# State-space outputs beside the gate projections, five recurrence steps a round, and another order in the gate

## The chip, the cores and the metric

The kernel runs on one core of one Trainium2 chip. The metric is device time in microseconds of one execution; the median of three runs is compared. Everything is float32 at the borders; products run on TensorE with each operand split into a high and a low part in a reduced float format, three matmuls for one product.

## The reference

A block with pooling and sparse attention comes first, then a gated linear attention layer, then the state-space layer that this change touches (S = 1024 positions, inner width 2048 as 128 groups of 16 channels, 64 complex states a group):

```python
u, z = split(h @ w_in)                      # 2048 columns each
states = scan(lam_bar * state + B_bar u)    # 128 groups, 64 complex states, 1024 steps
y = Re(C states) + d_skip * u
y = gelu(y)
y = y * sigmoid(y @ w_glu + b_glu)
y = y * silu(z)
out = y @ w_out
```

## The kernel before

The sequence is cut into 128 chunks of 8 positions, and the 128 groups into 16 octets of 8 groups (`octet(o)`). For each octet four small matrices do the work: `w_mat` takes the inputs of a chunk to the state that the chunk adds, `kp_d` (the T pieces) gives the outputs that depend on the chunk's own inputs, the recurrence carries states over the 128 chunks, and `v_mat` takes the carried state to outputs. The tile `X` holds the states: 64 KB a partition, indexed by state (real and imaginary parts on the 128 partitions), chunk and group, so that one octet's elements for one chunk are 8 contiguous floats and the next chunk lies 512 bytes on.

The weights, the inputs and the states all come through one stream, `WStream` (lines 43 to 144). A piece is put in order, loaded by SyncE into one of three raw buffers, and split by `pump`: ScalarE casts the high part (L177), VectorE or GpSimd (`lo`) subtracts for the low part (L185). Split pieces stand in a ring of six, are taken in the order in which they were put, and are freed by `release`. A piece with a gate is not started before its gate is true. All engines take their instructions in the order written; nothing is reordered.

`s5` (L2125) has these stages.

- The first loop, 19 rounds. Round i projects columns i of `w_in` (`project`: 48 matmuls 512 wide in two halves, evacuated by ScalarE at L2154) and, from round 3 on, does octet i - 3 (`states`: 24 matmuls 128 wide with `w_mat`, evacuated into `X` at L2196, then 24 with T, evacuated at L2204 and stored in `yp_d`). Rounds 16 to 18 already project the first three column blocks of z, with SiLU in the evacuation, stored in `z_d`.
- The recurrence, a generator on VectorE (`scan`, L2213) for four octets at a time, 29 steps each: three that only wait for a load, 15 over chunks within a segment, 4 that carry the ends of segments, 7 that correct a segment each. `scan_on(n)` writes n steps into the program; the first loop writes 4 a round from round 7 on.
- The second loop, 13 rounds, the other column blocks of z: one projection and `scan_on(6)` each. The products with `v_mat` come after it.
- The third loop, 16 rounds, one octet each. It takes a `v_mat` piece and the split states of the octet (the `X` piece), does 24 matmuls 128 wide into a two-bank PSUM tile (`big`, two of them), adds the stored part (VectorE, L2361), does the GELU (ScalarE, L2366), and for the octet two rounds back `y_out`: 8 transposes (L2316) into two PSUM banks, evacuated by ScalarE (L2317) and VectorE (L2319, L2320), half of it stored in `y_d`. From octet 10 on the first GLU accumulator is built beside it (`glu_early`).
- The GLU for the first half of the positions, 16 blocks of 48 matmuls, each followed by the sigmoid (L2467), the products and the split into `q_hi`, `q_lo`; `gate` (L2399) makes y times SiLU(z) one block ahead. Then the output projection, then the same for the second half.

Of the kernel before, what the change touches and what calls it, by code (L numbers as in the profile page):

```python
# [2087 lines left out]
def s5_pieces(g):  # L2088

    A, ws = g.A, g.ws  # L2090
    w_in = A["s5_w_in_2"][0]
    q = Ctx()
    q.u_d = u_d = g.dram.tile([8, 16, P, P], F, name="su_d")
    q.spilled = spilled = [False] * S5_NO
    q.octet = octet = lambda o: slice(o * 8, o * 8 + 8)

    def put_u(o):
        return ws.put(8, P, [((slice(None),) * 3, u_d.rearrange("t i g c -> (t i) g c")[:, octet(o), :])],
                      gate=lambda: spilled[o], lo="dve")

    def put_T(o):
        kp = g.kp_d
        src = []
        for t in range(8):
            src.append(((slice(t * 16, t * 16 + 16), slice(None), slice(None)),
                        bass.AP(tensor=kp.tensor, offset=kp.offset + o * 8 * 3840 + (7 - t) * 16,
                                ap=[[240, 16], [3840, 8], [1, P]])))
        return ws.put(8, P, src, lo="pool")

    def put_m(m, o, lo=None):  # L2110
        return ws.put(8, P, [((slice(None),) * 3, m[:, octet(o), :])], lo=lo)

    def put_cols(w, nk, c0, lo=None):
        return [ws.put(8, P, [((slice(None),) * 3, g.kview(w, k0 * P, 8, c0, P))], lo=lo) for k0 in range(0, nk, 8)]

    q.put_m, q.put_cols = put_m, put_cols
    q.first = []
    for i in range(S5_NO + S5_LAG):
        px = [put_u(i - S5_LAG), put_m(g.w_mat, i - S5_LAG, "pool"), put_T(i - S5_LAG)] if i >= S5_LAG else None
        q.first.append((i, px, put_cols(w_in, 8, i * P, "dve" if i == 1 else "pool")))  # L2120
    q.second = [(i, put_cols(w_in, 8, 2048 + i * P, "pool")) for i in range(S5_LAG, S5_NO)]
    return q


def s5(g, xn3, xstack, out):  # L2125
# [1 line left out]
    w_glu = A["s5_w_glu_2"][0]  # L2127
    w_out = A["s5_w_out_2"][0]
    NO, LAG = S5_NO, S5_LAG
    EARLY, GLU_AT, GLU_N = 1, (8, 14), 2  # L2130
    q = g.pieces.pop("s5") if "s5" in g.pieces else s5_pieces(g)
    u_d, spilled, octet, put_m, put_cols, first, second = (
        q.u_d, q.spilled, q.octet, q.put_m, q.put_cols, q.first, q.second)

    z_d = g.dram.tile([NO, P, S], F, name="sz_d")
    yp_d = g.dram.tile([NO, P, S], F, name="syp_d")
# [10 lines left out]
    def project(i, ids):  # L2147

        W = ws.take(ids)
        stage = stg.tile([P, S], F, name="w4")  # L2150
        for half in range(2):
            ps = g.bank()
            gemm_tr(g, hT, half, W, 0, P, ps, ids if half else None, True, later)
            nc.scalar.activation(half_of(stage, half, True), ps.rearrange("p (t c) -> p t c", t=8),  # L2154
                                 AF.Copy if i < NO else AF.Silu)
            ws.pump(1)
            if half == 0:
                yield
        if i >= NO:
            nc.sync.dma_start(z_d[i - NO], stage)  # L2160
            return
        for j in range(8):
            nc.sync.dma_start(u_d[:, :, i * 8 + j, :].rearrange("t i c -> i t c"),
                              stage[j * 16:j * 16 + 16, :].rearrange("p (t c) -> p t c", t=8))
        spilled[i] = True
# [10 lines left out]
    xstack.close()  # L2176
    X = pool_of(g, xp, "s5x").tile([P, P, P], F, name="X")
    nc.gpsimd.memset(X[:, 0], 0.0)
    third, pglu, pout = [], [[[] for _ in range(EARLY)], []], []
    for o in range(NO):  # L2180
        if o in GLU_AT:
            for e in range(EARLY):
                pglu[0][e] += put_cols(w_glu[GLU_AT.index(o) * 1024:], 8, e * P)
        third.append([put_m(g.v_mat, o, "dve" if o > 3 else "pool"),
                      ws.put(8, P, X[:, :, octet(o)].rearrange("p n g -> p g n"), gate=lambda o=o: scanned[o // 4])])
    for half in range(2):
        pglu[half] += [put_cols(w_glu, 16, e * P) for e in range(len(pglu[half]), NO)]
        pout.append([ws.put(1, S, [((slice(None),) * 3, g.kview(w_out, k * P, 1, 0, S))]) for k in range(16)])
# [1 line left out]
    def states(o, ids):  # L2190

        U, W = ws.take(ids[:2])
        ps = g.big().rearrange("p (g n) -> p g n", g=8)
        for j in range(8):
            g.mm3(ps[:, j], [a[:, j, :] for a in W], [a[:, j, :] for a in U], True, True)
        nc.scalar.copy(X[:, 1:P, octet(o)], ps.rearrange("p g n -> p n g")[:, 0:P - 1])  # L2196
        del ps
        yield
        T = ws.take(ids)[2]
        yp = stg.tile([P, 8, 8, 16], F, name="w4")  # L2200
        ps = g.big().rearrange("p (g n) -> p g n", g=8)
        for j in range(8):
            g.mm3(ps[:, j], [a[:, j, :] for a in U], [a[:, j, :] for a in T], True, True)
        nc.scalar.copy(yp.rearrange("c t g o -> c g t o"), ps.rearrange("c g (t o) -> c g t o", t=8))  # L2204
        del ps
        ws.release(ids)
        nc.sync.dma_start(yp_d[o], yp.rearrange("c t g o -> c (t g o)"))
        ws.pump(2)

    G4, J = 32, 16  # L2210
# [66 lines left out]
    for i, px, pp in first:  # L2277
        gens = [states(i - LAG, px)] if px else []
        gens.append(project(i, pp) if i else begun)
        for _ in range(2):  # L2280
            for ge in gens:
                next(ge, None)
                scan_on(1)
        if px and (i - LAG) % 4 == 3:
            scans.append(((i - LAG) // 4, scan((i - LAG) // 4)))
    per = 6
    ws.hi_eng, ws.lo_eng = ["act"], ["pool"]
    early = []
    for i, ids in second:
        if i == NO - 1:  # L2290
            for o in range(2):
                early.append(stg.tile([P, 8, P], F, name="w4"))
                nc.sync.dma_start(early[o], yp_d[o].rearrange("c (t x) -> c t x", t=8))
        for _ in project(NO + i, ids):
            pass
        scan_on(per)
    assert not scans
    hold.clear()
    hp.close()

# [3 lines left out]
    y_hl = ypool.tile([P, NO, 2, 512], R, name="y_hl")  # L2304
    y_hi, y_lo = y_hl[:, :, 0], y_hl[:, :, 1]
    wpool = pool_of(g, xp, "s5w", bufs=2)
    ypend = deque()

    def load_yp(o):
        nc.sync.dma_start(f32(y_hl[:, o]), yp_d[o].rearrange("c (a x) -> c a x", a=2))  # L2310

    def y_out():
        o, ya = ypend.popleft()
        pb = [g.bank(), g.bank()]
        for t in range(8):
            nc.tensor.transpose(pb[t // 4][:, t % 4 * P:(t % 4 + 1) * P], ya[:, t], g.ident)  # L2316
        nc.scalar.copy(y_hi[:, o], pb[0])  # L2317
        stage = wpool.tile([P, 512], F, name="w2")
        nc.vector.tensor_copy(stage, pb[1])  # L2319
        nc.vector.tensor_tensor(y_lo[:, o], pb[0], f32(y_hi[:, o]), OP.subtract)  # L2320
        nc.sync.dma_start(y_d[o], stage)

    accs, glu_w, glu_k = {}, {}, [0] * EARLY

    def glu_step(half, e, k, ps):

# [4 lines left out]
        if k % 8 == 7:  # L2331
            ws.release(ids)

    def glu_early(last, n):
        for e in range(EARLY):
            for _ in range(n):
                k = glu_k[e]
                if k > last:
                    break
                if k == 0:  # L2340
                    accs[e] = g.bank()
                glu_step(0, e, k, accs[e])
                glu_k[e] += 1

    AHEAD = 3
    ws.hi_eng, ws.lo_eng = ["act"], ["pool"]
    for o in range(2, AHEAD):
        load_yp(o)
    ws.pump(ws.RING)
    ws.age = 1  # L2350
    for o in range(NO):
        V, X_ = ws.take(third[o])
        ya = early[o] if o < 2 else stg.tile([P, 8, P], F, name="w4")
        if len(ypend) > 1:
            y_out()
        ps = g.big()
        for j in range(8):
            g.mm3(ps[:, j * P:(j + 1) * P], [b[:, j, :] for b in X_], [b[:, j, :] for b in V], True, True)
        part = ya.rearrange("c t x -> c (t x)") if o < 2 else f32(y_hl[:, o]).rearrange("c a x -> c (a x)")
        y4, part = [a.rearrange("c (t g o) -> c t g o", t=8, g=8) for a in (ya.rearrange("c t x -> c (t x)"), part)]  # L2360
        nc.vector.tensor_tensor(y4, part, ps.rearrange("c (g t o) -> c t g o", g=8, t=8), OP.add)  # L2361
        ws.release(third[o])
        ws.pump(3)
        if o >= GLU_AT[0] + 2:
            glu_early(o - 3, GLU_N)
        nc.scalar.activation(ya, ya, AF.Gelu_apprx_tanh)  # L2366
        ypend.append((o, ya))
        if o + AHEAD < NO:
            load_yp(o + AHEAD)
    glu_early(NO - 3, NO)  # L2370
    y_out()
    y_out()
    xp.close()
    ws.age = 0
    ws.hi_eng, ws.lo_eng = ["act"], ["pool", "dve"]
# [21 lines left out]
        return t  # L2397

    def gate(e, t):  # L2399
        nc.vector.tensor_tensor(t[:, 0], f32(y_hi[:, e]), f32(y_lo[:, e]), OP.add)  # L2400
        g.tt("dve" if e % 2 else "pool", t[:, 0], t[:, 0], t[:, 1], OP.mult)

    def finish(row, a, jk):

# [45 lines left out]
    for half in range(2):  # L2450
        hs = slice(half * 512, half * 512 + 512)
        gate(0, zs[0])
        for e in range(NO):
            k0 = glu_k[e] if half == 0 and e < EARLY else 0
            ps = accs.pop(e) if k0 else g.bank()
            for k in range(k0, 16):
                if k == 8:
# [112 lines left out]
```

## Time and profile before

| | |
|---|---|
| median of three runs | 2659.3 us (2655.4 to 2661.73) |
| the profiled execution | 2654.64 us, of which the span of the trace is 2652.9 us |
| busy in that span: TensorE, VectorE, ScalarE, GpSimd | 92%, 63%, 43%, 39% |
| mean granted clock of TensorE in that span | 0.958 of full speed |
| the first loop's rounds with states begin | about 1606 us into the span |
| first product with `v_mat` | 2014.2 us |
| the third loop's last chain piece ends in the GLU | 2122 us |

TensorE's matmuls overlap, so that a busy share near 100% still leaves room in the pipeline; the pace is better read from counts: a stretch that is full of 512-wide matmuls does one each 0.23 us. VectorE, ScalarE and GpSimd can be read as they stand. "Idle before" and the releaser say what an engine waited for.

### The profile page before, as it was taken

What the parts mean: (1) busy time and instruction counts of PE and PEld (TensorE: products, weight loads), DVE (VectorE), ACT (ScalarE), POOL (GpSimd) and SP (SyncE); (2) the same over time, 40 slices, a digit from 0 to 9 for tenths busy, and PEclk for the clock granted to TensorE, in tenths of its full rate; (3) what the DMA queues carried; (4) which work ended last, traced back from release to release, by engine and by line L of the source; (5) the groups of instructions that cost most, each with busy time, mean ns of one, the idle gap of its engine ahead of it and who ended that gap; (6) DMA issues with size and microseconds to landing.
All of it is one profiled execution on the core that took longest, in us unless ns stands there. A gap on an engine that the chain in (4) does not pass through costs nothing.

```text
span 2652.9 us, 33078 instructions
## 1 busy us (share of the span) xinstructions
PE 2440.0 (92%) x11817; PEld 1996.0 (75%) x11817; DVE 1675.6 (63%) x2970; ACT 1130.8 (43%) x1907; POOL 1024.5 (39%) x780
## 2 busy tenths in 40 slices
PE   5887976999999999998988899999996999999998
PEld 4665654787777777777777778888885888888887
DVE  5888676777454666785777750376998855425632
ACT  5458895556432222325434334444223832223321
POOL 3515553322201566663444414444322632332321
PEclk8998987899999999999988999999997899999999
DMA  8312124221333554545333217777433753444441
GB/s 266 105 36 70 50 84 140 84 65 54 117 115 103 141 144 144 160 153 177 119 104 109 78 61 196 199 192 202 143 98 106 248 152 118 147 139 139 147 139 56
DMA packets 330173, 338.25 MB, mean 127 GB/s; under 512 B 67366, under 2 KB 248182, under 8 KB 329752
## 3 DMA queue, kind: packets, MB, share of 16 engines
q1 hardware_dynamic: 330008, 336.13, 41.3%
q8 instruction: 93, 1.52, 0.2%
q14 instruction: 72, 0.59, 0.1%
HBM read 239.19 MB, written 96.87 MB: 127 GB/s over the span
## 4 chain that ended last, share of the span: by engine, by line
PE 63%; DVE 16%; ACT 8%; issue 7%; POOL 2%; DMA 2%; SPq 1%; DVEq 0%; ACTq 0%; POOLq 0%
PE mm L192 16%; PE mm L194 16%; PE mm L193 16%; PE big L194 3%; PE big L193 3%; PE big L192 3%; ACT tku L828 2%; PE big L1160 1%; PE mm L1675 1%; DVE whl L185 1%; DVE xacc L1988 1%; PE mm L1259 1%; DVE rs_t L213 1%; ACT tka_d L837 1%; POOL rs_h L210 1%
## 5 line engine op out<-in xcount | busy, mean ns | idle before, releaser
L185 POOL TENSOR_TENSOR whl<-wraw,whl 128x1024 fp32r<-128x1024 f32 x158 | 386.5, 2454 | 862.8 <-ACT whl L177 777.1
L177 ACT CAST whl<-wraw 128x1024 fp32r<-128x1024 f32 (+1 forms) x279 | 287.9, 1048 | 396.0 <-PE mm L194 265.2
L185 DVE TENSOR_TENSOR whl<-wraw,whl 128x1024 fp32r<-128x1024 f32 (+2 forms) x121 | 181.7, 1510 | 295.7 <-ACT whl L177 295.5
L192 PE MATMUL mm<-h_hi,whl 128*128 128x512 f32 x768 | 306.2, 399 | 3.8 <-ACT uT L966 2.3
L192 PE MATMUL mm<-whl,h_hi 128*128 128x512 f32 (+1 forms) x720 | 290.0, 403 | 16.7 <-ACT whl L177 11.6
L194 PE MATMUL mm<-h_hi,whl 128*128 128x512 f32 x768 | 302.5, 394 | 0.0
L193 PE MATMUL mm<-h_lo,whl 128*128 128x512 f32 x768 | 302.5, 394 | 0.0
L193 PE MATMUL mm<-whl,h_hi 128*128 128x512 f32 (+1 forms) x720 | 283.4, 394 | 7.7 <-DVE whl L185 7.7
L194 PE MATMUL mm<-whl,h_lo 128*128 128x512 f32 (+1 forms) x720 | 283.2, 393 | 0.0
L193 PE MATMUL mm<-y_hl,whl 128*128 128x512 f32 x512 | 202.9, 396 | 0.5 <-DVE y_hl L2320 0.5
L192 PE MATMUL mm<-y_hl,whl 128*128 128x512 f32 x512 | 203.2, 397 | 0.0
L194 PE MATMUL mm<-y_hl,whl 128*128 128x512 f32 x512 | 202.8, 396 | 0.0
L192 PEld LDWEIGHTS mm<-h_hi,whl 128*128 128x128 f32 x768 | 144.9, 189 | 41.2 <-ACT uT L966 3.5
L192 PEld LDWEIGHTS mm<-whl,h_hi 128*128 128x128 f32 x720 | 138.6, 192 | 45.2 <-ACT whl L177 12.0
L194 PEld LDWEIGHTS mm<-h_hi,whl 128*128 128x128 f32 x768 | 144.7, 188 | 33.0
L193 PEld LDWEIGHTS mm<-h_lo,whl 128*128 128x128 f32 x768 | 144.9, 189 | 31.3 <-issue 0.2
L193 PEld LDWEIGHTS mm<-whl,h_hi 128*128 128x128 f32 x720 | 138.6, 192 | 34.4 <-DVE whl L185 9.1
L194 PEld LDWEIGHTS mm<-whl,h_lo 128*128 128x128 f32 x720 | 137.7, 191 | 29.0
L185 DVE TENSOR_TENSOR w<-w 128x512 f32<-128x512 f32 x48 | 71.4, 1513 | 105.8 <-DMA w<-sz_d 61.2
L193 PEld LDWEIGHTS mm<-y_hl,whl 128*128 128x128 f32 x512 | 96.5, 188 | 23.9 <-DVE y_hl L2320 0.9
L194 PEld LDWEIGHTS mm<-y_hl,whl 128*128 128x128 f32 x512 | 96.4, 188 | 23.4
L192 PEld LDWEIGHTS mm<-y_hl,whl 128*128 128x128 f32 x512 | 96.5, 188 | 22.9
(540 smaller groups left out, 5831.2 us busy)
## 6 DMA issues: line engine op xcount, KB each, us to landing
wraw<-in_s_w_glu_dram SPq DMA_DIRECT2D x64, 512.0 KB, 4.0
wraw<-in_gla_w_in_dram SPq DMA_DIRECT2D x40, 512.0 KB, 3.7
wraw<-in_s_w_in_dram SPq DMA_DIRECT2D x32, 512.0 KB, 4.2
wraw<-in_s_w_out_dram SPq DMA_DIRECT2D x32, 512.0 KB, 3.5
gv_d<-stg SPq DMA_DIRECT2D x32, 256.0 KB, 2.2
v_mat<-vc SPq DMA_DIRECT2D x32, 256.0 KB, 2.6
w_mat<-wo SPq DMA_DIRECT2D x32, 256.0 KB, 2.4
gz_d<-stg SPq DMA_DIRECT2D x32, 256.0 KB, 2.1
```

What stands on the lines that cost most here:

```text
L177: nc.scalar.copy(out, in_)
L185: e.tensor_tensor(out, a, b, op)
L192: nc.tensor.matmul(out, lhsT=lhs[0], rhs=rhs[0], start=start, stop=False)
L193: nc.tensor.matmul(out, lhsT=lhs[0], rhs=rhs[1], start=False, stop=False)
L194: nc.tensor.matmul(out, lhsT=lhs[1], rhs=rhs[0], start=False, stop=stop)
L210: nc.gpsimd.tensor_tensor(h, v, self.mhalf[:, :n], OP.pow)
L213: nc.vector.tensor_tensor(t, h, h, OP.mult)
L828: nc.scalar.activation(aj[:, :(b + 1) * P], keys[b], AF.Sign, bias=abias[:, q:q + 1], accum_out=asum[:, q:q + 1])
L837: nc.scalar.activation(asgn[:, c], asum[:, c], AF.Sign, bias=aneed[:, c])
L1160: nc.tensor.matmul(ps[:, c0:c1], lhsT=qt[:, j, :], rhs=kT[:, h // 4, e, c0:c1], start=(e == 0), stop=(e == 1))
L1259: nc.tensor.transpose(ps[:, o:o + P], sms[e][:, jj * P:(jj + 1) * P], g.ident)
L1675: nc.tensor.matmul(ps[0:16, i * P:(i + 1) * P], lhsT=B1[:, g0 + i, :], rhs=vc[:, i, 0:8, :].rearrange("p k o -> p (k o)"), start=True, sto ...
```

## The change

Four things change, all in `s5_pieces` and `s5`.

- Twelve of the sixteen products with `v_mat` (`BESIDE = 12`) move into the second loop, one at the end of each of its first twelve rounds (`products`). The pieces are put in that order. One round later, `outputs` adds the stored part and writes the sum over the octet's states in `X`, and the GELU works in place there. The third loop does the last four octets, and `y_out` of all sixteen, three to a product; the transposes read `X` with 512 bytes from element to element. One in two of the second evacuations goes to ScalarE. The stored part has another order of its columns (`yp_d`), contiguous on its way out.
- The recurrence has five steps a round in the first loop (the `states` generator's second half is followed by two), and two and three in the halves of a second-loop round.
- The low part of the input pieces (`put_u`) goes to GpSimd instead of VectorE; the low part of the first twelve `v_mat` pieces goes to GpSimd (before: the first four).
- z is stored without SiLU. `gate` does a sigmoid (ScalarE), z times it (GpSimd) and the product with y (VectorE, before: in turn with GpSimd).

```diff
 def put_u(o):
         return ws.put(8, P, [((slice(None),) * 3, u_d.rearrange("t i g c -> (t i) g c")[:, octet(o), :])],
-                      gate=lambda: spilled[o], lo="dve")
+                      gate=lambda: spilled[o], lo="pool")
...
             nc.scalar.activation(half_of(stage, half, True), ps.rearrange("p (t c) -> p t c", t=8),
-                                 AF.Copy if i < NO else AF.Silu)
+                                 AF.Copy)
...
+    def put_out(o):
+        third.append([put_m(g.v_mat, o, "pool" if o < BESIDE else "dve"),
+                      ws.put(8, P, X[:, :, octet(o)].rearrange("p n g -> p g n"), gate=lambda: scanned[o // 4])])
+
+    for i in range(LAG, NO):
+        second.append((i, q.put_z(i)))
+        if i - LAG < BESIDE:
+            put_out(i - LAG)
+    for o in range(BESIDE, NO):
+        if o % 2 == 0:
+            pglu[0][0] += put_cols(w_glu[(o - BESIDE) * 512:], 8, 0)
+        put_out(o)
...
-        for _ in range(2):
+        for r in range(2):
             for ge in gens:
                 next(ge, None)
-                scan_on(1)
+                scan_on(1 + (r and ge is gens[0]))
...
+    def load_part(o):
+        parts[o] = stg.tile([P, S], F, name="w4")
+        nc.sync.dma_start(parts[o], yp_d[o])
+
+    def products(o):
+        V, X_ = ws.take(third[o])
+        ps = g.big()
+        for j in range(8):
+            g.mm3(ps[:, j * P:(j + 1) * P], [b[:, j, :] for b in X_], [b[:, j, :] for b in V], True, True)
+        ws.release(third[o])
+        ws.pump(2)
+        sums.append((o, ps))
+
+    def outputs():
+        o, ps = sums.popleft()
+        Xo = X[:, :, octet(o)]
+        gto = lambda a: a.rearrange("p (g t o) -> p g t o", g=8, t=8)
+        nc.vector.tensor_tensor(Xo.rearrange("p (g o) t -> p g t o", g=8), gto(parts.pop(o)), gto(ps), OP.add)
+        del ps
+        yield
+        nc.scalar.activation(Xo, Xo, AF.Gelu_apprx_tanh)
+
-    for i, ids in second:
...
-        for _ in project(NO + i, ids):
+    for n, (i, ids) in enumerate(second):
+        ge, ou = project(NO + i, ids), outputs() if sums else iter(())
+        next(ge)
+        next(ou, None)
+        scan_on(2)
+        for _ in ge:
             pass
-        scan_on(per)
+        for _ in ou:
+            pass
+        if n < BESIDE:
+            load_part(n)
+            products(n)
+        scan_on(3)
...
-            nc.tensor.transpose(pb[t // 4][:, t % 4 * P:(t % 4 + 1) * P], ya[:, t], g.ident)
+            nc.tensor.transpose(pb[t // 4][:, t % 4 * P:(t % 4 + 1) * P], X[:, :, o * 8 + t], g.ident)
         nc.scalar.copy(y_hi[:, o], pb[0])
         stage = wpool.tile([P, 512], F, name="w2")
-        nc.vector.tensor_copy(stage, pb[1])
+        g.copy("act" if o % 2 else "dve", stage, pb[1])
...
+    load_part(BESIDE)
+    done = 0
+    for o in range(BESIDE, NO):
+        if o + 1 < NO:
+            load_part(o + 1)
+        products(o)
+        ou = outputs()
+        for n in range(3):
+            y_out(done)
+            done += 1
+            next(ou, None)
+            ws.pump(1)
+            glu_early(2, done - 3)
+    while done < NO:
+        y_out(done)
+        done += 1
+        ws.pump(1)
+        glu_early(2, done - 3)
...
     def gate(e, t):
+        nc.scalar.activation(t[:, 0], t[:, 1], AF.Sigmoid)
+        g.tt("pool", t[:, 1], t[:, 1], t[:, 0], OP.mult)
         nc.vector.tensor_tensor(t[:, 0], f32(y_hi[:, e]), f32(y_lo[:, e]), OP.add)
-        g.tt("dve" if e % 2 else "pool", t[:, 0], t[:, 0], t[:, 1], OP.mult)
+        nc.vector.tensor_tensor(t[:, 0], t[:, 0], t[:, 1], OP.mult)
```

## Rows read from the trace of the kernel before

**Rows 1.** The page: busy time, share and instructions of each engine.
```profile
PE 2440.0 (92%) x11817; PEld 1996.0 (75%) x11817; DVE 1675.6 (63%) x2970; ACT 1130.8 (43%) x1907; POOL 1024.5 (39%) x780
```
**Rows 2.** Stretches: length, busy PE, PEld, DVE, ACT, POOL (instructions), clock, DMA share, GB/s.
```profile
1609.00:1857.00 248.00, 248.00 (x1443) 216.43 (x1442) 116.67 (x264) 106.84 (x123) 110.54 (x46) 1.00 0.71 195
1870.00:2014.00 144.00, 144.00 (x622) 116.89 (x621) 130.94 (x348) 29.39 (x39) 35.33 (x15) 1.00 0.36 113
2014.00:2041.00 27.00, 5.67 (x50) 5.49 (x48) 24.92 (x69) 6.75 (x5) 8.05 (x3) 0.64 0.05 22
2041.00:2122.00 81.00, 73.88 (x510) 70.10 (x510) 63.12 (x61) 65.69 (x63) 47.15 (x17) 0.85 0.77 250
2122.00:2284.00 162.00, 161.78 (x693) 130.23 (x694) 82.91 (x69) 49.30 (x60) 52.69 (x24) 1.00 0.44 132
```
**Rows 3.** Waits of PE from 2014 to 2123: total us, times, longest.
```profile
PE mm L2316 <- ACT w L2366: 27.9, 5, 23.7
```
**Rows 4.** Chain that ended last, 1550 to 2653: start, length, what.
```profile
1972.47 0.44 DVE mm L2237
...
1974.78 0.44 DVE mm L2237
...
2034.47 0.64 DVE mm L2261
...
2038.18 0.64 DVE mm L2261
...
2043.35 1.97 PE mm L2316 x8
...
2102.31 0.87 PE mm L2316 x8
...
2122.22 0.49 PE mm L193
```
**Rows 5.** PE in order of time from 2013: the first product with `v_mat`.
```profile
2014.20 0.22 PE L192 MATMUL big<-whl 128*128 128x128 f32 x1
```
**Rows 6.** Instructions on tile X: ns min/median/max, first and last start, forms.
```profile
L2240 DVE TENSOR_TENSOR X<-X,mm x88: 186/420/422, 1692.1 to 2014.5; 128x256 f32<-128x256 f32 x60, 128x32 f32<-128x32 f32 x28
...
L2196 ACT COPY X<-big x16: 992/998/1006, 1609.1 to 1856.8; 128x1016 f32<-128x1016 f32 x16
...
L185 POOL TENSOR_TENSOR whl<-X,whl x16: 2857/2920/3323, 1972.0 to 2109.0; 128x1024 fp32r<-128x1024 f32 x16
```
**Rows 7.** Groups of ScalarE by form, 2041 to 2122: busy us, mean ns, idle before.
```profile
L177 ACT CAST whl<-X 128x1024 fp32r<-128x1024 f32 x12 | 24.5, 2040 | 4.1 <-PE big L194 4.1
L177 ACT CAST whl<-wraw 128x1024 fp32r<-128x1024 f32 x19 | 19.8, 1055 | 5.1 <-issue 3.2 <-ACT y_hl L2317 1.0 <-DMA wraw<-in_s_w_glu_dram 0.9
L2366 ACT ACTIVATE w<-w 128x1024 f32<-128x1024 f32 x16 | 17.0, 1062 | 24.5 <-DVE w L2361 24.4
L2317 ACT CAST y_hl<-mm 128x512 fp32r<-128x512 f32 x16 | 9.2, 574 | 1.2 <-PE mm L2316 1.2
```
**Rows 8.** Groups of VectorE by form, 2041 to 2122.
```profile
L185 DVE TENSOR_TENSOR whl<-wraw,whl 128x1024 fp32r<-128x1024 f32 x12 | 25.4, 2113 | 2.0 <-ACT whl L177 1.9
L2361 DVE TENSOR_TENSOR w<-y_hl,big 128x1024 f32<-128x1024 f32 x14 | 16.9, 1210 | 3.3 <-PE big L194 3.3
L2320 DVE TENSOR_TENSOR y_hl<-mm,y_hl 128x512 fp32r<-128x512 f32 x16 | 10.9, 684 | 8.2 <-ACT y_hl L2317 8.2
```
**Rows 9.** GpSimd in one round of the first loop, in order of time.
```profile
1783.33 4.77 POOL L185 TENSOR_TENSOR whl<-wraw,whl 128x1024 fp32r<-128x1024 f32 x2 [6.28 <-ACT whl L177]
1790.79 2.41 POOL L185 TENSOR_TENSOR whl<-wraw,whl 128x1024 fp32r<-128x1024 f32 x1 [2.69 <-ACT whl L177]
```
**Rows 10.** ScalarE in order of time from 1780: the evacuation into X one round later.
```profile
1807.84 1.01 ACT L2196 COPY X<-big 128x1016 f32<-128x1016 f32 x1
```
**Rows 11.** Groups in the GLU, 2130 to 2400, by form: the sigmoid, the gate's product.
```profile
L2467 ACT ACTIVATE w<-mm,cols 128x512 f32<-128x512 f32 x17 | 11.6, 683 | 0.3 <-POOL w L185 0.3
...
L185 POOL TENSOR_TENSOR w<-w 128x512 f32<-128x512 f32 x9 | 14.4, 1602 | 11.7 <-DMA w<-sz_d 11.7
```

More of the change, by code (lines that the diff above doesn't have):

```diff
@@ L2120, in s5_pieces @@
         q.first.append((i, px, put_cols(w_in, 8, i * P, "dve" if i == 1 else "pool")))
-    q.second = [(i, put_cols(w_in, 8, 2048 + i * P, "pool")) for i in range(S5_LAG, S5_NO)]
+    q.put_z = lambda i: put_cols(w_in, 8, 2048 + i * P, "pool")
     return q
@@ L2129, in s5 @@
     NO, LAG = S5_NO, S5_LAG
-    EARLY, GLU_AT, GLU_N = 1, (8, 14), 2
+    BESIDE = 12
     q = g.pieces.pop("s5") if "s5" in g.pieces else s5_pieces(g)
-    u_d, spilled, octet, put_m, put_cols, first, second = (
-        q.u_d, q.spilled, q.octet, q.put_m, q.put_cols, q.first, q.second)
+    u_d, spilled, octet, put_m, put_cols, first = (
+        q.u_d, q.spilled, q.octet, q.put_m, q.put_cols, q.first)
     z_d = g.dram.tile([NO, P, S], F, name="sz_d")
@@ L2178, in s5 @@
     nc.gpsimd.memset(X[:, 0], 0.0)
[L2179 to L2185, printed above, removed]
+    second, third, pglu, pout = [], [], [[[]], []], []
+    def put_out(o):
[9 more added lines that the diff above has]
+        put_out(o)
     for half in range(2):
@@ L2199, in states @@
         T = ws.take(ids)[2]
-        yp = stg.tile([P, 8, 8, 16], F, name="w4")
+        yp = stg.tile([P, S], F, name="w4")
         ps = g.big().rearrange("p (g n) -> p g n", g=8)
@@ L2203, in states @@
             g.mm3(ps[:, j], [a[:, j, :] for a in U], [a[:, j, :] for a in T], True, True)
-        nc.scalar.copy(yp.rearrange("c t g o -> c g t o"), ps.rearrange("c g (t o) -> c g t o", t=8))
+        nc.scalar.copy(yp.rearrange("c (g x) -> c g x", g=8), ps)
         del ps
         ws.release(ids)
-        nc.sync.dma_start(yp_d[o], yp.rearrange("c t g o -> c (t g o)"))
+        nc.sync.dma_start(yp_d[o], yp)
         ws.pump(2)
@@ L2279, in s5 @@
         gens.append(project(i, pp) if i else begun)
-        for _ in range(2):
+        for r in range(2):
             for ge in gens:
                 next(ge, None)
-                scan_on(1)
+                scan_on(1 + (r and ge is gens[0]))
         if px and (i - LAG) % 4 == 3:
             scans.append(((i - LAG) // 4, scan((i - LAG) // 4)))
-    per = 6
-    ws.hi_eng, ws.lo_eng = ["act"], ["pool"]
-    early = []
-    for i, ids in second:
[L2290 to L2293, printed above, removed]
-        for _ in project(NO + i, ids):
-            pass
-        scan_on(per)
-    assert not scans
+    parts, sums = {}, deque()
+    def load_part(o):
[17 more added lines that the diff above has]
+        nc.scalar.activation(Xo, Xo, AF.Gelu_apprx_tanh)
+    ws.hi_eng, ws.lo_eng = ["act"], ["pool"]
+    for n, (i, ids) in enumerate(second):
[4 more added lines that the diff above has]
+        for _ in ge:
+            pass
+        for _ in ou:
[4 more added lines that the diff above has]
+        scan_on(3)
+    assert not scans and not sums
     hold.clear()
@@ L2306, in s5, with y_out @@
     wpool = pool_of(g, xp, "s5w", bufs=2)
[L2307 to L2313, printed above, removed]
+    def y_out(o):
         pb = [g.bank(), g.bank()]
         for t in range(8):
-            nc.tensor.transpose(pb[t // 4][:, t % 4 * P:(t % 4 + 1) * P], ya[:, t], g.ident)
+            nc.tensor.transpose(pb[t // 4][:, t % 4 * P:(t % 4 + 1) * P], X[:, :, o * 8 + t], g.ident)
         nc.scalar.copy(y_hi[:, o], pb[0])
         stage = wpool.tile([P, 512], F, name="w2")
-        nc.vector.tensor_copy(stage, pb[1])
+        g.copy("act" if o % 2 else "dve", stage, pb[1])
         nc.vector.tensor_tensor(y_lo[:, o], pb[0], f32(y_hi[:, o]), OP.subtract)
         nc.sync.dma_start(y_d[o], stage)
-    accs, glu_w, glu_k = {}, {}, [0] * EARLY
+    accs, glu_w = {}, {}
+    glu_k = [0]
     def glu_step(half, e, k, ps):
@@ L2332, in glu_step, with glu_early @@
             ws.release(ids)
[L2334 to L2348, printed above, removed]
+    def glu_early(n, last):
+        while n and glu_k[0] <= last:
+            if glu_k[0] == 0:
+                accs[0] = g.bank()
+            glu_step(0, 0, glu_k[0], accs[0])
+            glu_k[0] += 1
+            n -= 1
     ws.pump(ws.RING)
     ws.age = 1
[L2351 to L2372, printed above, removed]
+    load_part(BESIDE)
[16 more added lines that the diff above has]
+        glu_early(2, done - 3)
     xp.close()
@@ L2453, in s5 @@
         for e in range(NO):
-            k0 = glu_k[e] if half == 0 and e < EARLY else 0
+            k0 = glu_k[0] if half == 0 and e == 0 else 0
             ps = accs.pop(e) if k0 else g.bank()
```

## The prediction

> **What bounds the kernel now.** I read the page's busy times first, then the stretches of the state-space layer, the waits of TensorE, the chain of waits, and last single groups of instructions. TensorE is busy 92% of the span [rows 1], so a change pays only where TensorE stands still or is clocked down. In the first loop, the second loop and the GLU it does neither: busy throughout, clock 1.00 [rows 2]. [...] The waits name the first gap: a transpose stood 23.7 us behind the GELU [rows 3], and the chain shows why: up to then it runs through the recurrence on VectorE, from 1972 on [rows 4]. VectorE was busy 131 of the second loop's 144 us and all of the gap [rows 2]. It had six steps a round, about 2.3 us each (1972.47 to 1974.78 [rows 4]), some 13.8 us against a round of 144.0/13 = 11.08 us on TensorE, and came out late.
>
> How much is lost there? Paces first. A 512-wide matmul takes 11.08/48 = 0.231 us. The first loop's rounds are (1856.8 - 1609.1)/15 = 16.51 us apart [rows 6]; less 11.08 for the projection, 48 matmuls 128 wide take 5.43 us: 0.113 each, 2.71 for an octet's 24. Eight transposes take 0.87 us [rows 4]. From 2014.2 [rows 5] to 2122.2 [rows 4] are 108.0 us. The work in them at full pace: 16 x 2.71 = 43.4 for the products, 16 x 0.87 = 13.9 for the transposes, and 14 steps of the first GLU accumulator, 42 x 0.231 = 9.7; together 67.0. So 41 us are lost, and no arrangement of the same matmuls can win more there.
>
> **The change, part by part.** *Products beside the projections.* No matmul is added or removed. The second loop gets 12 x 2.71 = 32.5 us of products: 144.0 + 32.5 = 176.5 us, a round of 13.8 us, if TensorE does not wait. Five steps of the recurrence are written in a round. In the first loop five long steps are 5 x 2.31 = 11.6 us of a 16.5 us round, where VectorE is now busy 117 of 248 us [rows 2]: hidden. Its 12 rounds now hold 60 steps, so two scans are done when the second loop begins, and 56 steps are left. A scan costs VectorE 15 x 2.31 in its long steps, 7 x (2038.18 - 2034.47 = 3.71) in its corrections [rows 4], and seven short turns of five instructions near 0.19 [rows 6], about 1.1 each: 34.7 + 26.0 + 7.7 = 68.4 us. Two scans are 137 us, and twelve adds come on top. The add read and wrote runs before, 1.21 us [rows 8]; now it writes with 512 bytes from element to element. The nearest row is the cast of an X piece, which reads with that step: 2.04 us against 1.055 for a contiguous one, 1.93 times [rows 7]. So the add takes 1.21 to 2.34 us, and the sum is 151 to 165 us of the 165.6 that twelve rounds last. It fits. The worst round is the eleventh: five corrections and an add, 19.8 to 20.9 us, end 6 to 11 us into the next round; the last step of the last scan then ends at the latest some 3 us into the thirteenth. The twelfth product is past; the thirteenth, first of the third loop, needs the cast (2.04) and the low part on GpSimd (2.92 [rows 6]) behind it, and is due at the end of that 11.1 us round: 3 us to spare. ScalarE meets that X cast one round early and holds the evacuation queued behind it; TensorE has a second bank for the next half. I allow 1 us for such joints. The other additions to a round lie below 13.8 us: ScalarE two casts of weights, one of X, two evacuations and a GELU, 2 x 1.055 + 2.04 + 2 x 0.6 + 1.06 (to 2.05) = 6.4 to 7.4 us; GpSimd three low parts, 2 x 2.41 [rows 9] + 2.92 = 7.7. SyncE gets one load of the stored part a round into the three stage buffers; it waits for a buffer last stored from, and before it on the queue stand the round's loads. Moved bytes are 2 MB in 13.8 us, about 150 GB/s, against 195 carried in the first loop [rows 2].
>
> *The third loop.* Left are 4 products, 10.8 us, the 14 accumulator steps, 9.7 us, and 16 times eight transposes. These now load their weights out of X with the 512-byte step. From below they cost 0.109 us each as now, 13.9 in all; from above I take the X cast's 1.93, so 0.21 each, 27.0 in all. GpSimd's subtraction for an X piece, 2.92 against 2.41, a factor of 1.2, lies between. [...] That makes 47.5 us of matmuls.
>
> [...]
>
> To the 47.5 come waits. ScalarE enters the third loop with an evacuation, a GELU, an X cast and about three casts of weights, 0.6 + 1.06 + 2.04 + 3.2 = 6.9 us, before it reaches the first `y_out` [rows 7]; TensorE has one product and two `y_out` to do, 2.7 + 2 x 1.7 = 6.1, and the third wants banks that come free at 6.9 + 0.57 + 0.68 = 8.2 us: 2.1 us lost. A round after that (a product, three `y_out`, three accumulator steps) is 2.7 + 5.1 + 2.1 = 9.9 us on TensorE. On ScalarE a GELU, an X cast, a cast or two of weights, three casts and one or two evacuations make 7 to 8 us; on VectorE the add, a low part at 2.11 and four or five evacuations at 0.68 [rows 8] make 6 to 7.5. Neither is the bound, but both run in order: I allow 0.7 us a round, 2.8 us. The third loop is then 47.5 + 4.9 = 52.4 us.
>
> *Low part of the inputs on GpSimd.* Sixteen times 2.41 us on GpSimd, 16 low parts less on VectorE. In a round GpSimd does two, ends at 1788.1, waits 2.69 us for the next cast and is done at 1793.2 [rows 9]; the inputs' low part fits that gap. TensorE wants the pair only for the 24 matmuls that end before 1807.8 [rows 10], so from about 1805. I cost it at nothing; without its cover it would be 2.41 us a round.
>
> *The gate.* Per block one more sigmoid on ScalarE, 0.683 us, one product on GpSimd, 1.6 us, every time [rows 11], and VectorE's second product always. A block is 11.1 us of TensorE; ScalarE is busy 49, GpSimd 53, VectorE 83 us in 162 while TensorE is full [rows 2]. The sigmoid of z waits for its load, and behind it on ScalarE stand the sigmoid of the block and later casts; six split pieces, three blocks, cover that. Nothing; uncovered, 32 x 0.683 = 22 us.
>
> *The sum.* Before: 144.0 + 108.0 = 252.0 us. After: 176.5 + 1 + 52.4 = 229.9. Gain 22 us. The profiled execution took 2654.64 us and would take 2632.6; it lies 4.7 us under the median of 2659.3, from which the same gain gives 2637.3 us.
>
> **The rivals.** *A strided load of weights costs TensorE nothing.* Then the third loop holds 34.4 us of matmuls, and ScalarE, with about 35 us of its own there, is as long; with 10 us of waits 44.4, gain 30, time 2629. For it: TensorE's rows nowhere show such a price. Against it: the X cast's.
>
> *The clock falls in the third loop.* It fell where TensorE stood 23.7 us [rows 2, 3], and the 81 us after it had 0.85. With 47.5 us of work at 0.85 the loop is 8 us longer, at 0.70 20 us: 2645 to 2657, say 2650. Against it: no such standstill leads into it now.
>
> *The first loop starves (the other side).* Four low parts a round queue on GpSimd, 9.6 us of 16.5, and hold the three raw buffers longer, so later loads start later. If the whole low part came onto TensorE's path in 16 rounds, that is 38.6 us: 2637 + 39 = 2676, slower. It decides from 22/16 = 1.4 us a round. For it: the casts there wait for loads. Against it: the 11 us between 1793.2 and 1805 [rows 9, 10].
>
> **How the numbers follow.** The forecast 0.46, own range 2629 to 2646; free loads 0.28; clock 0.13; starved first loop 0.06; anything else, on either side, 0.07. A measurement of this kernel tells 0.2%, 5.3 us, from no change. The clock case falls half into faster, a third into the same, the rest beyond; so faster 0.87, same 0.06, slower 0.07. The range goes from 2621 (third loop without strided price and almost without waits) to 2652 (the clock case's middle).
>
> **What would show it.** Right: PE without waits in the second loop at 13.8 us a round, no gap after it, eight transposes near 1.7 us, a third loop of about 52 us, first-loop rounds still 16.5 us apart. Wrong: waits of PE for X pieces, transposes at 0.87 us, a clock under 0.9 in the third loop, or rounds of 18 us in the first.

## The result, and the profile after

The changed kernel takes 2697.1 us (median of 4; 2695.5 to 2699.5), the one before 2657.4: a ratio of 1.0145, 95% interval 1.0133 to 1.0157. It is slower by 40 us; 2637 us had been forecast, 22 us faster. The spans of the two profiled executions are 2693.7 and 2652.9 us.

Stretches of the kernel after, columns as in [rows 2], which hold their counterparts:

```profile
1609.00:1857.00 248.00, 248.00 (x1444) 216.44 (x1443) 137.19 (x347) 107.02 (x122) 145.35 (x62) 1.00 0.72 197
1870.00:2014.00 144.00, 144.00 (x745) 121.29 (x744) 125.22 (x271) 62.87 (x62) 79.91 (x32) 1.00 0.50 159
2014.00:2041.00 27.00, 26.84 (x141) 22.32 (x139) 25.13 (x61) 4.99 (x6) 7.66 (x4) 1.00 0.37 116
2041.00:2064.00 23.00, 9.30 (x42) 7.84 (x42) 15.80 (x33) 8.27 (x8) 4.76 (x2) 0.70 0.20 66
2064.00:2120.00 56.00, 43.57 (x259) 39.36 (x258) 26.91 (x31) 30.27 (x39) 21.55 (x9) 0.94 0.64 203
...
2284.00:2300.00 16.00, 9.01 (x37) 6.65 (x36) 7.38 (x10) 6.82 (x9) 4.87 (x3) 0.81 0.23 82
...
2460.00:2500.00 40.00, 32.34 (x129) 25.77 (x128) 16.79 (x26) 9.94 (x16) 10.75 (x10) 0.87 0.46 138
...
2580.00:2620.00 40.00, 22.99 (x87) 17.60 (x87) 13.41 (x14) 11.81 (x16) 9.70 (x5) 0.74 0.49 175
```

Before, in the same columns, from the end of the first half's blocks almost to the last matmul:

```profile
2284.00:2644.00 360.00, 360.00 (x1566) 293.77 (x1564) 145.66 (x161) 97.03 (x127) 102.00 (x56) 1.00 0.41 129
```

The first loop is as forecast. The second loop is full (745 matmuls in 144 us, 622 before) until 2041, when TensorE stops and stands for 13.9 us. The third loop ends at 2118, so second and third loop together gained about 3.5 us (2118.7 against 2122.2). The new losses lie where before there were none: behind 2284, in the GLU's second half and in both output projections, each stretch with a lower clock. The last matmul ends at 2685.1, 566 us after the third loop; before it ended at 2644.2, 522 us after: 44 us are lost there.

The waits of TensorE from 1600 on say for what it stood (before, there was one of this size [rows 3] and none behind 2123):

```profile
PE mm L192 <- ACT w L2492: 33.4, 7, 10.2
PE mm L192 <- DVE mm L2268: 13.9, 1, 13.9
PE mm L2348 <- DVE w L179: 5.6, 3, 2.7
PE mm L2348 <- DVE y_hl L2352: 3.5, 1, 3.5
PE mm L2348 <- ACT w L177: 3.4, 4, 1.5
```

L2492 is the sigmoid of a GLU block, which frees that block's PSUM bank; L2268 is the recurrence; L2348 are the third loop's transposes. ScalarE, VectorE and SyncE in two GLU blocks of the kernel after, each in order of time:

```profile
2164.68 0.63 ACT L2423 ACTIVATE w<-w 128x512 f32<-128x512 f32 x1 [4.91 <-DMA w<-sz_d]
2165.21 0.67 ACT L2492 ACTIVATE w<-mm,cols 128x512 f32<-128x512 f32 x1
2168.77 0.62 ACT L2494 CAST q_hi<-w 128x512 fp32r<-128x512 f32 x1 [2.89 <-DVE w L185]
2169.30 1.99 ACT L177 CAST whl<-wraw 128x1024 fp32r<-128x1024 f32 x2
2176.48 0.63 ACT L2423 ACTIVATE w<-w 128x512 f32<-128x512 f32 x1 [5.19 <-DMA w<-sz_d]
```
```profile
2170.38 1.23 DVE L185 TENSOR_TENSOR whl<-wraw,whl 128x1024 fp32r<-128x1024 f32 x1 [0.26 <-ACT whl L177]
```
```profile
2162.36 9.63 SPq L100 DMA_DIRECT2D wraw<-in_s_w_glu_dram  x2
2172.05 0.57 SPq L2419 DMA_DIRECT2D w<-sz_d  x1
2173.88 9.91 SPq L100 DMA_DIRECT2D wraw<-in_s_w_glu_dram  x2
2183.84 0.58 SPq L2419 DMA_DIRECT2D w<-sz_d  x1
```

It is a closed ring of waits, 11.8 us round (2164.68 to 2176.48), while TensorE's block takes 11.2. Behind ScalarE's sigmoid of z (2164.68) come the block's own sigmoid, the products on GpSimd and VectorE, the cast `q_hi`, and behind it the casts of weights. VectorE's low part of the first of these weights (2170.38 to 2171.61) frees a raw buffer; the weight load that has waited for that buffer goes, and behind it on SyncE the next z load (2172.05). That lands, and ScalarE's next sigmoid of z starts (2176.48).

Before, VectorE or GpSimd waited for z. What ScalarE's casts of weights waited for last was TensorE (4.6 us for one of a block's two casts, 0.2 to 0.8 for the other), and z's loads came at TensorE's pace, 11.2 us apart:

```profile
2167.83 1.05 ACT L177 CAST whl<-wraw 128x1024 fp32r<-128x1024 f32 x1 [4.55 <-PE mm L194]
```
```profile
2164.98 0.57 SPq L2396 DMA_DIRECT2D w<-sz_d  x1
...
2176.18 0.57 SPq L2396 DMA_DIRECT2D w<-sz_d  x1
```

A ring slower than TensorE cannot make up a lag. The first half's first sigmoid starts some 12 us behind its block's matmuls (before: 7), and its last one still 11.5 us behind (before: 1.0). The output projection, which wants the PSUM banks that the sigmoids free, takes 97.1 us instead of 87.1. The second half loses more: its 16 blocks take 192.1 us (179.2 before) and its output projection 108.9 (87.2), with the last sigmoid 24.0 us behind. In its first blocks the stores and loads of the first half's last rows stand on SyncE ahead of the z load, which itself waits up to 3.8 us for a store out of its stage buffer, so that ScalarE waits 9.5 to 13.3 us for z, four times:

```profile
2463.91 1.02 SPq L2440 DMA_DIRECT2D out_dram<-w  x2
2464.97 0.46 SPq L2454 DMA_DIRECT2D w<-x_d  x1
2467.19 0.33 SPq L2419 DMA_DIRECT2D w<-sz_d  x1
```
```profile
2471.30 0.63 ACT L2423 ACTIVATE w<-w 128x512 f32<-128x512 f32 x1 [12.48 <-DMA w<-sz_d]
```

Before, a block's sigmoid that came 19.1 us after the one ahead was followed by the next after 4.0; now 19.1 is followed by 11.5.

VectorE and ScalarE around the second loop of the kernel after:

```profile
1871.51 2.02 DVE L185 TENSOR_TENSOR whl<-X,whl 128x1024 fp32r<-128x1024 f32 x1 [13.58 <-ACT whl L177]
...
1890.53 1.98 DVE L2315 TENSOR_TENSOR X<-w,big 128x1024 f32<-128x1024 f32 x1 [7.66 <-DMA w<-syp_d]
```
```profile
2030.17 1.07 ACT L2318 ACTIVATE X<-X 128x1024 f32<-128x1024 f32 x1 [9.84 <-DVE X L2315]
...
2055.72 1.98 ACT L177 CAST whl<-X 128x1024 fp32r<-128x1024 f32 x1 [22.11 <-DVE X L2269]
2057.61 0.59 ACT L2154 ACTIVATE w<-mm 128x512 f32<-128x512 f32 x1
```

VectorE stood 13.6 us for one X piece's low part and 7.7 us for a load. The last correction ended at 2055 and not at about 2038. The last projection's second half waits for VectorE (it uses a PSUM bank that the recurrence had held), and ScalarE's X cast waits for the same end, with an evacuation behind it.

Instructions on X after, beside [rows 6, 7, 8]:

```profile
L2348 PEld LDWEIGHTS mm<-ident,X x128: 220/254/268, 2064.7 to 2117.3; 128*128 128x128 f32 x128
...
L2269 DVE TENSOR_TENSOR X<-X,mm x56: 653/653/655, 1734.0 to 2054.7; 128x480 f32<-128x480 f32 x56
...
L2315 DVE TENSOR_TENSOR X<-w,big x16: 1861/1984/2344, 1890.5 to 2102.1; 128x1024 f32<-128x1024 f32 x16
L2318 ACT ACTIVATE X<-X x16: 1050/1060/1383, 1896.8 to 2104.1; 128x1024 f32<-128x1024 f32 x16
```

### The profile page after: what moved, and what is told of

Its sections match the earlier page's. It is cut to its first block, busy times and chain, and to the rows that moved or that the text cites. A ratio compares the mean times of both kernels' runs of the same rounds, so it can differ in the third digit from the quotient of the medians.

```text
span 2693.7 us, 33083 instructions
## 1 busy us (share of the span) xinstructions
PE 2447.2 (91%) x11817; PEld 1996.2 (74%) x11817; DVE 1614.2 (60%) x2954; ACT 1148.6 (43%) x1946; POOL 1098.2 (41%) x820
## 5 line engine op out<-in xcount | busy, mean ns | idle before, releaser
L185 POOL TENSOR_TENSOR whl<-wraw,whl 128x1024 fp32r<-128x1024 f32 x183 | 445.0, 2440 | 753.9 <-ACT whl L177 639.1
L192 PE MATMUL mm<-h_hi,whl 128*128 128x512 f32 x768 | 307.7, 401 | 17.7 <-DVE mm L2268 13.9
L192 PE MATMUL mm<-whl,h_hi 128*128 128x512 f32 (+1 forms) x720 | 290.0, 403 | 13.9 <-ACT whl L177 10.1
L185 DVE TENSOR_TENSOR whl<-wraw,whl 128x1024 fp32r<-128x1024 f32 (+2 forms) x96 | 133.2, 1397 | 134.6 <-ACT whl L177 134.5
L2425 DVE TENSOR_TENSOR w<-y_hl 128x512 f32<-128x512 f32 x32 | 24.3, 760 | 214.1 <-POOL w L185 214.1
L192 PEld LDWEIGHTS mm<-y_hl,whl 128*128 128x128 f32 x512 | 98.0, 191 | 32.7 <-ACT w L2492 10.8
```

Of the source, the lines that this page charges most:

```text
L185: e.tensor_tensor(out, a, b, op)
L192: nc.tensor.matmul(out, lhsT=lhs[0], rhs=rhs[0], start=start, stop=False)
```

## The experiments

Times are medians; the kernel before stood at 2656 to 2659 us beside them. Gains are counted from the changed kernel's 2697.1, which was not measured again beside them, so that gains of 3 us are no more than that spread. The theory: two separate losses, the gate's ring through SyncE's queue, and VectorE's lateness in the second loop.

**gate_alone**, the gate on the kernel before.
```diff
-  AF.Copy if i < NO else AF.Silu)
+  AF.Copy)
 def gate(e, t):   # as in the change
```


> The kernel before with the gate part of the change alone: z stored without SiLU, sigmoid of z and two products in the gate. Theory G: the loss behind 2120 us is all the gate's, so 2657 + 42 = 2699 us, blocks of the first half 11.8 us apart on ScalarE. Rival S: the loss there needs the other parts (the pieces' place in the ring or in the raw buffers at the start of the GLU): within 10 us of 2657.

It took 2708.4 us, a ratio of 1.0185 (1.0170 to 1.0200): 49.5 us are lost, and the first half's blocks are again 11.7 us apart. In its trace 45 us of them lie behind the third loop, as in the changed kernel, and 3 in the third loop, for a reason that stays open. The gate alone does it; rival S falls.

**silu_back**, the gate part undone in the changed kernel.
```diff
-  AF.Copy)
+  AF.Copy if i < NO else AF.Silu)
 def gate(e, t):   # as before the change
```


> The changed kernel with the gate part undone: SiLU in z's evacuation, the gate as it was before. Theory G (the new gate costs some 45 us behind 2120 us, the recurrence's place the rest): 2697 - 45 = 2652 us, GLU blocks 11.1 us apart, no PE wait for the block's sigmoid; in the second loop ScalarE loads a table twice a round, 2 x 1.28 us, without effect on PE unless its queue is the bound there. Rival S (the loss in the GLU comes of the pieces' place at its start): 2690 us or more.

It took 2654.4 us, a ratio to the kernel before of 0.9989 (0.9977 to 1.0001): 42.7 us are back, and no wait for the block's sigmoid is left. The stand of 13.8 us at 2047 stays; the other three parts of the change together give nothing that can be told from zero.

**gate_late**, the same work in another order.
```diff
-                gate(e + 1, zs[0])
             nc.scalar.activation(t[:, 1], ps, AF.Sigmoid, ...)
...
             g.sub("dve", q_lo[:, e], t[:, 0], f32(q_hi[:, e]))
+            if e + 1 < NO:
+                gate(e + 1, zs[0])
```


> The changed kernel with one move: the gate of the next block (sigmoid of z, its product, the product with y) is written behind the block's own sigmoid and split, not ahead of them. Same work. Theory G: in the changed kernel ScalarE and VectorE do block e's sigmoid and products behind the wait for z of block e+1, the weight casts stand behind those, SyncE's next z load behind the raw buffers that the casts free; this ring takes 11.8 us a block where TensorE takes 11.1. Without the block's own 4 us in it the ring is under 11.1 us and the GLU costs what it did before: 2697 - 42 = 2655 us, PE never waits for the sigmoid in the GLU. [...]

It took 2680.5 us, 17 us back and not the 42 of theory G. The ring did not open; ScalarE's sigmoids of z were still 11.85 us apart (2164.06, 2175.91), since z's load still stood behind the weight loads and VectorE's product with z, 2.84 us beside GpSimd's subtraction, now stood ahead of the block's sigmoid. Most of what it gained lies in the second half's blocks: they took 179.2 us, as before the change, and not 192.1. The block's sigmoid there no longer stood behind the long waits for the next z; both output projections stayed as slow (99.0 and 107.9 us).

**z_early**, the place of the z load alone.
```diff
             k0 = glu_k[0] if half == 0 and e == 0 else 0
+            ahead = e + 1 < NO and (half == 0 or e > 8)
+            if ahead:
+                zs.append(load_z(half, e + 1))
...
-                zs.append(load_z(half, e + 1))
+                if not ahead:
+                    zs.append(load_z(half, e + 1))
```


> The changed kernel with the new gate kept, but z of the next block loaded at the start of a block (all of the first half, the blocks after the ninth of the second), ahead of the loads of weights that it stands behind on SyncE. Theory Q (the ring runs through SyncE's queue: casts free raw buffers, the next weight load, then the z load, then ScalarE's sigmoid of z and the next casts): the first half's blocks fall to 11.1 us, the stand of PE at 2284 us (7 to 9 us) goes, and of the second half's losses about half: 2697 - 20 to - 35 = 2662 to 2677 us. Rival W (amount of work): no change.

It took 2665.2 us, 32 us back, with all of the added work in place: theory Q holds, rival W falls. In the first half ScalarE no longer waits for z, and the sigmoids are 11.15 us apart:

```profile
2169.03 0.63 ACT L2423 ACTIVATE w<-w 128x512 f32<-128x512 f32 x1
2169.56 0.67 ACT L2496 ACTIVATE w<-mm,cols 128x512 f32<-128x512 f32 x1
...
2180.18 0.63 ACT L2423 ACTIVATE w<-w 128x512 f32<-128x512 f32 x1
```

Both output projections take 87 to 88 us again. What is still lost lies in the second half's blocks, 191.0 us against 179.2, most of which kept the load where it was.

**six_steps**, more of the recurrence in the first loop.
```diff
-                scan_on(1 + (r and ge is gens[0]))
+                scan_on(1 + r)
```


> The changed kernel with six steps of the recurrence in a first-loop round instead of five: 72 instead of 60 written before the second loop. Theory V: the stand of TensorE at 2041 to 2064 us comes of VectorE, which is late with the last scan by about 20 us; twelve steps of 2.3 us less in the second loop end that, PE waits no more there, 2697 - 20 = 2677 us. Rival A: TensorE stands for ScalarE, whose queue of casts and evacuations is too long whatever VectorE does: within 4 us of 2697. Rival F: six steps, 13.9 us of a 16.5 us round, delay the first loop: its rounds get longer than 16.5 us.

It took 2693.8 us, 3 us back: a miss. The last scan ended 26 us earlier (2029; 35 us earlier if counted from the first round with states, which came 9 us later in this trace). But TensorE now stood there, 9.9 us, for the bank of the recurrence: five corrections a round, 18.6 us, and an add, in 13.8 us, made VectorE late all the same. The first loop stayed full.

**xlow_part**, VectorE's two idle times taken away.
```diff
-  gate=lambda: scanned[o // 4])])
+  gate=lambda: scanned[o // 4], lo="pool")])
...
+    load_part(0)
     for n, (i, ids) in enumerate(second):
...
-            load_part(n)
+            if n:
+                load_part(n)
```


> The changed kernel with the low part of every X piece on GpSimd (one of them stood on VectorE and held it 13.6 us) and the stored part of octet 0 loaded ahead of the second loop (VectorE waited 7.7 us for it). Theory V: these two idle times made VectorE late; the last scan ends some 20 us earlier and TensorE's stand at 2041 goes: 2697 - 20 = 2677 us. Rival C: twelve rounds of five steps and a 2.0 us add are too much for VectorE in any case: the gain stays under 8 us.

It took 2694.4 us, 2.7 back, as rival C has it; TensorE's stand stayed at 13.9 us. VectorE stood for the next things instead, 8.6 us for the scan's load, 8.0 for GpSimd's read of the octet that the add overwrites, 6.0 for the product.

**add_contig**, the stride moved from VectorE to ScalarE.
```diff
-        nc.vector.tensor_tensor(Xo.rearrange("p (g o) t -> p g t o", g=8), gto(parts.pop(o)), gto(ps), OP.add)
+        part = parts.pop(o)
+        nc.vector.tensor_tensor(part, part, ps, OP.add)
...
-        nc.scalar.activation(Xo, Xo, AF.Gelu_apprx_tanh)
+        nc.scalar.activation(Xo.rearrange("p (g o) t -> p g t o", g=8), gto(part), AF.Gelu_apprx_tanh)
```


> The changed kernel with one edit: the add of the stored part is written in place, contiguous, and the GELU writes X with the 512-byte step. The add falls from 1.98 to 1.21 us if the step is its price. Theory V: 12 x 0.77 = 9 us less on VectorE up to the end of the last scan, which bounds TensorE: 2697 - 9 = 2688 us. Rival: the step costs ScalarE as much (2.05 us for 1.06) and it is the bound: no gain.

It took 2691.7 us, 5.4 of 9 back.

**steps_only**, six steps a first-loop round and four a second-loop round.
```diff
-                scan_on(1 + (r and ge is gens[0]))
+                scan_on(1 + r)
...
-        scan_on(3)
+        scan_on(2)
```


> The changed kernel with the steps alone moved: six a first-loop round, four a second-loop round; the strided add, the low part on VectorE and the late load stay. If it is the bursts of five corrections ahead of an add that hold ScalarE and TensorE, this gives most of the 18 us that all four edits gave: 2697 - 14 to - 18 = 2679 to 2683 us. If the other three edits do the work, it stays near the six steps' 2694.

It took 2684.0 us, 13.1 back, 1 us short of the least that was expected; the wait for the recurrence is down to 2.7 us.

**scan_plan**, these steps with xlow_part and add_contig.

> The changed kernel, gate as changed, with all that relieves VectorE in the second loop: six steps a first-loop round, four a second-loop round, the add written contiguous in place (the GELU on ScalarE now writes X with the 512-byte step), X pieces' low parts on GpSimd, octet 0's stored part loaded ahead. Theory V (an add that stands behind corrections on VectorE holds the GELU on ScalarE, and behind it the evacuations and TensorE): at most seven corrections lie in less than two rounds, PE's waits of 10 to 14 us there and the clock's fall go, the third loop starts near 2049 us instead of 2064: 2697 - 16 = 2681 us. Rival A (ScalarE's own work, now with a strided GELU of 1.06 to 2.05 us): PE still waits for evacuations, within 5 us of 2694.

It took 2679.4 us, 17.7 back; TensorE waits no more in the second loop, and the first transposes come at 2049.8 (2064.7). The strided GELU takes 2.06 us, the contiguous add 1.22.

**tr_contig**, transposes of a constant; it leaves the outputs out of all that follows.
```diff
-  X[:, :, o * 8 + t], g.ident)
+  g.ident, g.ident)
```


> The changed kernel whose transposes read a contiguous constant in place of the outputs in X (so the outputs are left out of what follows). If the 512-byte step is what makes eight transposes take about 1.06 us instead of 0.8, they fall back to 0.8 and the third loop is some 4 us shorter: 2693 us. By the forecast's price (0.21 us each) it would be 13 us. If the transposes' pace comes of something else, it stays at 1.06.

It was timed once, at 2692.7 us, so that the price is read from the trace. The weight loads, then eight transposes and the matmul after them, here and in the kernel after:

```profile
L2348 PEld LDWEIGHTS mm<-ident x128: 138/141/231, 2068.7 to 2117.6; 128*128 128x128 f32 x128
```
```profile
2093.10 1.06 PE L2348 MATMUL mm<-ident 128*128 128x128 f32 x8
2093.91 0.48 PE L192 MATMUL mm<-y_hl,whl 128*128 128x512 f32 x1
```
```profile
2092.34 1.30 PE L2348 MATMUL mm<-ident,X 128*128 128x128 f32 x8
2093.40 0.48 PE L192 MATMUL mm<-y_hl,whl 128*128 128x512 f32 x1
```

From start to next start it is 0.81 against 1.06 us: the 512-byte step costs 0.25 us for eight, 4 us in all.

**best_silu** is scan_plan with the gate undone; **best_z** is scan_plan with z loaded at the start of each block of both halves, and the late work of the first half moved there with it:
```diff
             k0 = glu_k[0] if half == 0 and e == 0 else 0
+            for _ in range(2):
+                next(rest, None)
+            if e + 1 < NO:
+                zs.append(load_z(half, e + 1))
...
-            for _ in range(2):
-                next(rest, None)
             if e + 1 < NO:
-                zs.append(load_z(half, e + 1))
                 gate(e + 1, zs[0])
```


> The changed kernel with the gate part undone (SiLU at z's evacuation) and everything that relieves VectorE in the second loop (six steps, then four; contiguous add; X low parts on GpSimd; octet 0's part ahead). If the two losses are separate, the gains add: 2697 - 43 - 18 = 2636 us, 0.8% under the kernel before. If the two table loads a round (2.6 us) and the strided GELU (2.06 us) on ScalarE together hold the evacuations, PE waits for them in the second loop and the sum stays above 2645.

> The same second loop with the new gate kept, and in both halves z of the next block loaded at the start of a block (the late work of the first half moved with it). Theory Q (the ring through SyncE's queue is the whole of the gate's loss): no PE wait for the block's sigmoid in either half, 2697 - 45 - 18 = 2634 us. If the new gate costs something besides the place of the load, the second half still loses some of its 12 us: 2640 to 2650.

They took 2637.3 us, a ratio to the kernel before of 0.9920 (0.9906 to 0.9933), and 2636.9 us, 0.9917 (0.9902 to 0.9932): both beat both kernels, and the gains add. In the second half of best_z, load and late work moved together, so what each is worth there is not shown. TensorE's waits in best_z from 1600 on are these, all in the third loop:

```profile
PE mm L2351 <- ACT w L177: 3.3, 3, 1.9
PE mm L2351 <- DVE w L179: 2.4, 2, 1.3
```

## Why the prediction was wrong

*The gate at nothing* is the step that turned the sign. It counted work (0.68 us on ScalarE, 1.6 on GpSimd) against TensorE's 11.1 us a block and took the six split pieces for cover of the wait. The work came out no larger (0.63 and 1.3 us); what failed is that the wait was closed into a ring with its own cause. Before, VectorE or GpSimd waited for z while ScalarE's casts went by TensorE's pace; now ScalarE waits, and the casts that let the next z load go stand behind it. A buffer of three blocks covers a wait that comes once, not a ring that takes 11.8 us where TensorE takes 11.2: no lag is made up in it, neither that with which the first half begins nor those of the late work in the second. Cost: 42.7 us by silu_back, 49.5 by gate_alone; in the changed kernel's trace 10 us behind the first half and 35 in and behind the second. The price named for lost cover, 22 us, was of the work and so too low. z_early shows the load's place on SyncE as the cause in the first half; the share of the late work in the second half's 35 us stays open.

*"It fits" for VectorE* was the second step that failed. Steps and adds had the forecast sizes (the add took 1.98 us, within 1.21 to 2.34), and 151 to 165 us in 165.6 was taken for enough. It left no room for what VectorE stands for in order: a low part that the alternating choice put on it, a load, the read that the add overwrites. No single one was the cause (xlow_part, add_contig gave 3 and 5 us); with fewer corrections a round the stand shrank to 2.7 us (steps_only, 13.1 of the 17.7 us), and with all edits it went (scan_plan). So of the forecast gain 17.7 us were lost here.

*The third loop* was forecast at 52.4 us and took 56 (2062 to 2118), of other parts. The strided transposes cost 4 us more than contiguous ones and not 13, nearer to the rival's nothing than to the forecast. Waits and slow matmuls cost 18.5 us and not 4.9 (56 less 10.8, 9.7 and 17.0 for matmuls); 12.5 of them are waits of the transposes. The 27.0 us in the forecast's 47.5 were taken from ScalarE's cast (1.93 times); that the price of that cast holds for TensorE was the author's estimate, and no run shows it. The load's own record rose 1.8 times (0.254 us against 0.141), but the pace only 1.3 times (1.06 us against 0.81 for eight), as loads overlap (0.13 us from one transpose to the next, with a load of 0.254 each).

*Right*: first-loop rounds of 16.4 us ((1855.9 - 1609.9)/15), GpSimd's low parts there hidden, products at 13.8 us a round, no low clock before the stand. The rival of a starved first loop fell; none of the rivals had the ring. With both losses taken away the kernel takes 2637 us, the forecast's number, and the second loop's part of that estimate held (products 13.9 us apart in best_z). The third loop's part is luck: it took 52 us in best_z, as forecast, but with some 37.5 us of matmuls and 14.7 of waits and slow pace, where 47.5 and 4.9 had been summed. And best_silu and best_z have edits that the change did not have.

With 512 bytes from element to element the add took 1.98 us (changed kernel) against 1.22 without (scan_plan), the GELU 2.06 (scan_plan) against 1.06 (changed kernel), the weight load 0.254 (changed kernel) against 0.141 (tr_contig). On TensorE most of the load's price was hidden: 0.113 us more a load, 0.25 us more for eight transposes.

## What to carry to other kernels

Before a wait is costed at nothing, follow what stands behind it on its engine round to the wait's own cause. If the wait gates the next load that it will wait for, compare the ring's period with that of the engine that bounds the kernel, not the work; a ring slower than that engine (here 11.8 us against 11.2) keeps every lag that it meets. Issue a load that nothing gates ahead of loads that wait for buffers on the same queue (z_early, 32 us). An engine filled to its sum (here VectorE, by the forecast 151 to 165 us of 165.6) needs slack for in-order waits: give bursts of long steps fewer places in the tight stage and more in the loose one (steps_only, 13.1 us).

## What was not expected of the hardware

TensorE's stand cost more than its length: after 13.9 us of standing the first matmuls went at 0.43 us each for some 3.5 us, where they went at 0.23 ahead of it, and the mean granted clock was 0.70 from 2041 to 2064; after the stands behind 2284 the granted clock was lower too, 0.74 from 2580 to 2620. And VectorE's product of two SBUF operands took 2.84 us beside GpSimd's subtraction (gate_late) and 0.69 without it (changed kernel).
